# Delta net front: keys and queries side by side in one tile, one product of 256 columns for both

## The chip, the cores and the metric

The kernel runs on one core of a Trainium2 chip. Its time is the device time of one launch in microseconds (us): the median of three runs before the change is 1162.49 us (1161.85 to 1162.65). The engines of a core each run their own queue of instructions in order and wait for each other by semaphores: PE (matrix products), DVE (vector), ACT (scalar functions), POOL (GpSimd), SP (which issues DMAs here).

## What is computed

One residual block: a layer norm, a mixer of two branches with gates, a second norm, and a mixture of experts. The change lies in the second branch, a gated delta net with 8 heads of 128 channels over 512 positions. For each head, keys, queries and values are projections of the normed input, each through a causal convolution of four taps and a SiLU. The reference, cut to what matters here:

```
qkv = jax.nn.silu(_causal_dwconv(dn_qkv, dn_conv_w))
q, k, vv = jnp.split(qkv, [DN_KEY, 2 * DN_KEY], axis=-1)
...
kk = jnp.einsum('bhnik,bhnjk->bhnij', k, k)
lmat = jnp.where(strict, beta[..., :, None] * kk * decay, 0.0)
amat = jnp.eye(CHUNK) + lmat
sol = lax.linalg.triangular_solve(amat, rhs, left_side=True, lower=True, unit_diagonal=True)
attn = jnp.einsum('bhnik,bhnjk->bhnij', q, k) * decay
...
v_new = uu - ww @ state
o = qd @ state + aa @ v_new
state = state * cd + kd.T @ v_new
```

So two products have the keys as one factor: keys with keys, which gives the matrix to invert, and keys with queries, which gives the attention inside a chunk. The kernel takes chunks of 128 positions, four per head.

## The kernel before

The program is cut into parts whose instructions are recorded first and then put in order: the norm and the gated spatial branch with the decays; the delta net; the merge; then routing and the experts, which are written in their final order. The change touches the delta net alone.

In that part, `front(h)` prepares a head and `chain(h)` solves and steps through its chunks. The loop over heads records `front(h + 1)` and then `chain(h)`, so that one head is prepared while the other is stepped. Six gate projections for the merge are recorded behind everything (`gates_b`), and each has to follow the first operation of head 7's chain, which reads Lx and thus L:

```
rec.rank, rec.after, rec.after_on = 2 * H, rec.ops[first], ("PE", "ACT", "SP")
kk.gates_b(TG, range(2, 8))
```

A projection (`proj`) is 24 products of 128 x 512 named psi in the trace. Its weights come as one 512 KB transfer `raw`, which ACT rounds to `hi` and DVE subtracts to `lo`; of `raw` there are three buffers, of `hi` and `lo` two. `conv` copies the projection out (`xp`), multiplies and adds the taps (`acc`, three times on DVE), and ACT applies SiLU into `kT`, `qT` or `kr`.

`front` then, for the keys: transposes them (`pk<-ident,kT`, `tr4`), takes sums of squares (`ssk`), scales (`kd`), and computes factors on POOL (`rk`, `cb`, and the decay matrix `DL`). Four products `pkk` of keys with keys (in the trace pk<-kT) times DL give `L`. From L come Lx (four copies on POOL), Ld, Lc, Le on DVE, the product `pl` (pk<-Le), Lb on ACT, and fourteen short steps on DVE (pr and U8, both in the trace as pr and U) that invert blocks of 8, then U and Uc, and the transposition `pu` of Uc. Behind that in the record stand the queries: projection, convolution, transposition, ssq, rq, the products `paq` (pk<-qT,kT) and `aT`; last the values. `chain` doubles the inverted blocks (tiles B, pz, pt, Z, Tc, Ud, Td, then Z6 and T6), and then steps through four chunks: p1 (state with keys and queries), R, p2 with U, V, p4 with kd, Sn, p3 with aT (in the trace all p), o.

What sets the order is a planner: `Rec.order` runs through a list of all recorded operations, with a cost for each, and places on the engine that is free first what is ready, by rank (`2h + 2` for a front, `2h + 1` for a chain, one more for projections) and then by the place in the record. On PE it keeps to one kind, wide (projections) or not, while something of it is ready, with at most six wide ones in a row when another kind waits. Every engine then runs its own list in that order. PSUM has one bank for the front (pool PF, tag pf, in the trace pk), two for projections, two for pz and pt, three for the steps.

Of the kernel before, what the change touches and what calls it, by code (L numbers as in the profile page):

```python
# [16 lines left out]
F32 = mybir.dt.float32  # L17
# [4 lines left out]
AF = mybir.ActivationFunctionType  # L22
OP = mybir.AluOpType
# [27 lines left out]
C_BU, C_BQ, C_BK, C_BV, C_BZ, C_BGA, C_BGB = (8 * i for i in range(7))  # L51
# [9 lines left out]
def bc(ap, n, at):  # L61

    dims = [list(d) for d in ap.ap]
    dims.insert(at, [0, n])
    return bass.AP(tensor=ap.tensor, offset=ap.offset, ap=dims)
# [255 lines left out]
class K:  # L321
# [384 lines left out]
    def conv(self, W, ps, tileno, bcol, out):  # L706

        nc, c = self.nc, self.c
        col = lambda i: c["cols"][:, i:i + 1]
        xp = self.xp[self.nxp % 2]  # L710
        self.nxp += 1
        nc.scalar.activation(out=xp[:, 3:515], in_=ps, func=AF.Identity, bias=col(bcol))
        cw = C_CONV + 4 * tileno
        acc = W.tile([128, T], F32, name="acc")
        nc.scalar.activation(out=acc, in_=xp[:, 3:515], func=AF.Copy, scale=col(cw + 3))
        for j in (2, 1, 0):
            nc.vector.scalar_tensor_tensor(out=acc, in0=xp[:, j:j + 512], scalar=col(cw + j), in1=acc,
                                           op0=OP.mult, op1=OP.add)
        nc.scalar.activation(out=out, in_=acc, func=AF.Silu)

    def front(self, h, W, W1, PF):


        nc, c = self.nc, self.c
        v, act, te = nc.vector, nc.scalar, nc.tensor
        hc = lambda name: c[name][:, :, h]
        f2 = lambda t: t.rearrange("p j n -> p (j n)")

        def wide(name):
            return PF.tile([128, 4, 128], F32, name=name, tag="pf")  # L730

        def full(name, pool=W):
            return pool.tile([128, 4, 128], F32, name=name)
# [5 lines left out]

        base = 25 + 4 * h  # L740
        s = {"h": h}
        s["kT"] = kT = full("kT")
        self.conv(W, self.proj(base + 2), 8 + h, C_BK + h, f2(kT))
        pk = wide("pk")
        self.tr4(pk, kT)
        ssk = W.tile([128, 4], F32, name="ssk")
# [10 lines left out]
        s["nc"] = cb[:, 2]  # L757
        DL = self.DL[h]
        nc.gpsimd.tensor_tensor(out=DL, in0=DL, in1=bc(cb[:, 1], 128, 2), op=OP.mult)
        pkk = wide("pkk")  # L760
        for j in range(4):
            te.matmul(pkk[:, j], kT[:, j], kT[:, j], start=True, stop=True)
        s["L"] = L = full("L")
        v.tensor_tensor(out=L, in0=pkk, in1=DL, op=OP.mult)

        s["Lx"] = Lx = W.tile([128, 4, 32], F32, name="Lx")
        for i in range(4):
# [11 lines left out]
        Le = W1.tile([128, 4, 8, 8], F32, name="Le")  # L779
        v.tensor_tensor(out=Le, in0=bc(Lc, 8, 2), in1=bc(bc(c["del8"], 8, 2), 4, 1), op=OP.mult)  # L780
        pl = wide("pl")
        plf = f2(pl)[:, 0:256]
        te.matmul(plf, c["blk8"], Le.rearrange("p t i j -> p (t i j)"), start=True, stop=True)
        Lb = W1.tile([128, 4, 8, 8], F32, name="Lb")
        act.copy(out=Lb.rearrange("p t i j -> p (t i j)"), in_=plf)
# [2 lines left out]
        for j in range(7):  # L788
# [5 lines left out]
                        in1=bc(c["blk8"].rearrange("p (b i) -> p b i", i=8), 4, 1), op=OP.mult)  # L794
        s["Uc"] = Uc = W.tile([128, 4, 32], F32, name="Uc")
        v.tensor_tensor(out=Uc.rearrange("p t (b i) -> p t b i", i=8), in0=bc(U8, 4, 2),
                        in1=bc(c["blk8c"].rearrange("p (b i) -> p b i", i=8), 4, 1), op=OP.mult)
        pu = wide("pu")
        te.transpose(pu[:, 0], f2(Uc), c["ident"])
        s["Tc"] = Tc = W.tile([128, 128], F32, name="Tc")  # L800
        act.copy(out=Tc, in_=pu[:, 0])
        s["qT"] = qT = full("qT")
        self.conv(W, self.proj(base + 1), h, C_BQ + h, f2(qT))
        pq = wide("pq")
        self.tr4(pq, qT)
        ssq = W.tile([128, 4], F32, name="ssq")
# [2 lines left out]
        v.tensor_scalar(ssq, ssq, 128.0, 128.0 * L2_EPS, op0=OP.mult, op1=OP.add)  # L809
        s["rq"] = rq = W.tile([128, 4], F32, name="rq")  # L810
        nc.gpsimd.tensor_tensor(out=rq, in0=ssq, in1=c["mhalf"][:, 0:4], op=OP.pow)
        paq = wide("paq")
        for j in range(4):
            te.matmul(paq[:, j], kT[:, j], qT[:, j], start=True, stop=True)
        s["aT"] = aT = full("aT")
        v.tensor_tensor(out=aT, in0=paq, in1=self.DA[h], op=OP.mult)
        vr = full("kr")
        self.conv(W, self.proj(base), 16 + h, C_BV + h, f2(vr))
        pv = wide("pv")
        self.tr4(pv, vr)  # L820
        s["vb"] = vb = full("vb")
# [1159 lines left out]
def build(nc, tc, a):  # L1981
# [70 lines left out]
    TG = pool("tg")  # L2052
    PF, PW, PS = pool("pf", 1, space=PSUM), pool("pw", 2, space=PSUM), pool("ps", 1, space=PSUM)
    front, chain = (Static(HW, 2), Static(HW1), Static(PF)), (Static(PW, 2), Static(PS))
    kk.tgs = []
    st = kk.front(0, *front)
    rec.rank = 2.5
    kk.gates_b(TG, range(0, 2))
    for h in range(H):

        rec.rank = 2 * h + 2
        nxt = kk.front(h + 1, *front) if h + 1 < H else None
        rec.rank = 2 * h + 1
        first = len(rec.ops)
        kk.chain(st, *front, *chain)
        zeros.append(rec.sync.dma_start(out=y_dram[h * 128:(h + 1) * 128, :].rearrange("p (a n) -> p a n", a=4),
                                        in_=bc(zero, 4, 1)))
        st = nxt
# [192 lines left out]
```

## Time and profile before

| | |
|---|---|
| median of 3 runs | 1162.49 us (1161.85 to 1162.65) |
| time of the profiled execution | 1165.03 us |
| its span | 1163.2 us |
| PE busy | 1033.1 us (89%), 7046 products |
| DVE busy | 633.9 us (54%) |
| ACT busy | 369.2 us (32%) |
| POOL busy | 215.5 us (19%) |
| HBM read and written | 273.74 MB and 21.00 MB |

The profile is of one execution. A row of the timeline gives the start in us from the span's start, the duration, the engine, the line of the kernel (all recorded operations have one line, L275), the operation, the tile written and the tiles read, the part of PE's array, the shape, how many in a row, and in brackets how long the engine idled before it and what it waited for. Matmuls are pipelined, so that starts, not durations, tell what one costs; a product in 32-bit floats shows as two rows (two passes), a transposition and a psi as one. In a table of windows a row gives the stretch, its length, the busy time of PE, of PE's weight loads, DVE, ACT and POOL, the share of the clock that PE was granted, the DMA share and GB/s. In a group's row stand the count, the busy time and the mean in ns, and the idle time before.

### The profile page before, as it was taken

Reading aid. Unit: us, or ns where it says so; the run is one execution under the profiler, and the core shown is the slowest. Engines: PE = TensorE matmul, PEld = TensorE weight load, DVE = VectorE, ACT = ScalarE, POOL = GpSimd, SP = SyncE. Lnnn points to the kernel's source line nnn. Section 1 sums busy time; section 2 is a strip of 40 time slices with the busy share of each in tenths; the row PEclk is TensorE's granted clock in tenths of the full one; section 3 lists DMA queues with packets and bytes.
Section 4 is the critical chain, followed back from the end, with each engine's and each line's share of the span. In section 5 each row is a group of like instructions: output and inputs, shape, how many; then the busy total and the mean of one; then the engine's idle time right before and its main releaser. Section 6 shows DMA issues by size and latency. Waiting matters only on the chain. (4 is left out here: it accounts for less than half of the span.)

```text
span 1163.2 us, 18964 instructions
## 1 busy us (share of the span) xinstructions
PE 1033.1 (89%) x7046; PEld 684.4 (59%) x7046; DVE 633.9 (54%) x1435; ACT 369.2 (32%) x818; POOL 215.5 (19%) x291
## 2 busy tenths in 40 slices
PE   5999999999999999999999987798788787978754
PEld 4888788877777777777888753343333433333321
DVE  8575444477678677863485755354434432222156
ACT  6343346444544555443533122112111111110110
POOL 3010100032212222120100112224122222121110
PEclk9999999999999999998999999999999998998955
DMA  5412432711121121111647399999999999999996
GB/s 215 152 71 75 160 109 93 235 56 55 56 73 51 60 65 61 57 56 40 240 178 307 140 380 395 396 396 388 408 374 410 393 408 386 418 388 408 414 418 245
DMA packets 56210, 268.35 MB, mean 231 GB/s; under 512 B 10867, under 2 KB 15251, under 8 KB 32288
## 3 DMA queue, kind: packets, MB, share of 16 engines
q1 hardware_dynamic: 44400, 246.96, 55.4%
q0 software_dynamic: 9104, 14.87, 3.8%
q10 hardware_dynamic: 2592, 4.99, 1.2%
q8 instruction: 73, 1.20, 0.4%
q14 instruction: 41, 0.34, 0.1%
HBM read 273.74 MB, written 21.00 MB: 253 GB/s over the span
## 5 line engine op out<-in xcount | busy, mean ns | idle before, releaser
L275 PE MATMUL psi<-hTh,hi 128*128 128x512 f32 x448 | 184.8, 415 | 0.0
L275 PE MATMUL psi<-hTh,lo 128*128 128x512 f32 x448 | 180.8, 404 | 0.3 <-DVE lo L275 0.3
L275 PE MATMUL psi<-hTl,hi 128*128 128x512 f32 x448 | 180.6, 404 | 0.0
L275 DVE TENSOR_TENSOR lo<-raw,hi 128x1024 fp32r<-128x1024 f32 x74 | 92.5, 1250 | 75.2 <-ACT hi L275 75.0
L1768 PE MATMUL us<-raw,xs 128*32 128x256 f32 x1296 | 90.1, 418 | 33.5 <-DMA raw<-in_w 24.0
L1784 DVE TENSOR_TENSOR h<-h,us 128x128 f32<-128x128 f32 x32 | 9.2, 288 | 191.7 <-ACT h L1783 181.2
L275 ACT CAST hi<-raw 128x1024 fp32r<-128x1024 f32 x74 | 77.4, 1046 | 107.3 <-PE psi L275 89.3
L275 PEld LDWEIGHTS psi<-hTl,hi 128*128 128x128 f32 x448 | 84.7, 189 | 20.8 <-issue 3.0
L275 PEld LDWEIGHTS psi<-hTh,hi 128*128 128x128 f32 x448 | 84.8, 189 | 20.3 <-issue 3.3
L275 PEld LDWEIGHTS psi<-hTh,lo 128*128 128x128 f32 x448 | 85.0, 190 | 18.5 <-issue 1.8
L1768 PEld LDWEIGHTS us<-raw,xs 128*32 128x32 f32 x1296 | 42.6, 117 | 75.9 <-issue 25.5
L1768 PE MATMUL u<-raw,x 128*64 128x512 f32 x304 | 72.6, 620 | 10.0 <-PEq L1684 4.1
L1812 POOL DMA_INDIRECT y_rows<-once,itail x28 | 25.3, 903 | 240.5 <-DVE once L1832 207.6
L1783 ACT ACTIVATE h<-us 128x128 f32<-128x128 f32 x32 | 8.9, 277 | 187.2 <-PE us L1768 118.2
L275 DVE SCALAR_TENSOR_TENSOR acc<-xp,cols,acc 128x512 f32<-128x512 f32 x72 | 53.9, 749 | 5.3 <-ACT acc L275 4.3
L1793 ACT COPY hT<-t 128x128 f32<-128x128 f32 x32 | 8.5, 266 | 151.0 <-PE t L1790 144.1
L1768 PEld LDWEIGHTS u<-raw,x 128*64 128x64 f32 x304 | 22.8, 141 | 53.2 <-issue 49.5
L1832 DVE COPY once<-yz 32x256 f32<-32x256 f32 x112 | 46.7, 417 | 13.4 <-DMA y_rows<-once,itail 6.8
L1805 PE MATMUL yz<-raw,hT 128*32 128x256 f32 x576 | 43.8, 447 | 8.3 <-DMA raw<-in_w 5.5
L275 POOL TENSOR_TENSOR rk<-ssk,mhalf 128x4 f32<-128x4 f32 x8 | 10.0, 1251 | 177.9 <-DVE ssk L275 177.9
L1698 POOL DMA_INDIRECT mh<-h_dram,idx x36 | 35.1, 975 | 40.8 <-issue 22.6
L1805 PE MATMUL y<-raw,hT 128*64 128x512 f32 x160 | 38.0, 620 | 5.2 <-PEq L1684 2.4
(544 smaller groups left out, 1979.0 us busy)
## 6 DMA issues: line engine op xcount, KB each, us to landing
raw<-in_w SPq DMA_DIRECT2D x147, 1024.0 KB
raw<-in_wt SPq DMA_DIRECT2D x73, 512.0 KB
rawl<-in_w SPq DMA_DIRECT2D x22, 1024.0 KB
rawh<-in_w SPq DMA_DIRECT2D x22, 1024.0 KB
raw<-in_wv SPq DMA_DIRECT2D x8, 512.0 KB
y_rows<-zero SPq DMA_DIRECT2D x8, 512.0 KB
rawl<-in_wo SPq DMA_DIRECT2D x3, 1024.0 KB
vt<-in_x SPq DMA_DIRECT2D x4, 512.0 KB
```

Source lines behind the costliest of these rows:

```text
L275: op._ins = getattr(getattr(self.nc, op.attr), op.name)(*map(real, op.args), **{k: real(x) for k, x in op.kw.items()})
L1698: self.nc.gpsimd.indirect_dma_start(out=x, out_offset=None, in_=self.h1_dram, in_offset=bass.IndirectOffsetOnAxis(ap=self.blocks[b][2 + i] ...
L1768: self.nc.tensor.matmul((self.end if p is None else self.u[:, p])[q * r:(q + 1) * r, 0:c], x[:, k, r0:r0 + r], self.raw[b, k // 2][:, o:o ...
L1783: self.nc.scalar.activation(out=h, in_=u, func=AF.Silu)
L1784: self.nc.vector.tensor_mul(out=h, in0=h, in1=w)
L1793: self.nc.scalar.copy(out=x[:, n], in_=self.t[1][:, 0:128])
L1805: self.nc.tensor.matmul(y[q * r:(q + 1) * r, 0:c], t[:, i, j * r:(j + 1) * r], self.raw[b, 4 + k // 2][:, o:o + c], start=k == 0, stop=k == 3)
L1812: x = self.nc.gpsimd.indirect_dma_start(out=out, out_offset=bass.IndirectOffsetOnAxis(ap=idx, axis=0), in_=src, in_offset=None, bounds_che ...
L1832: nc.vector.tensor_copy(out=small[:, q], in_=src)
```

## The change

Keys and queries of a head become the two halves of one tile `kq` of four chunks by two by 128, so that `kT` and `qT` are views of it. The queries' projection and convolution are recorded ahead of L. The eight products of 128 columns (pkk and paq) become four of 256 columns, two chunks in each of two PSUM tiles `pkq`; DVE takes L and aT from their halves, two chunks at a time. `conv` writes its result through a view by chunk.

```
-        nc.scalar.activation(out=out, in_=acc, func=AF.Silu)
+        nc.scalar.activation(out=out, in_=acc.rearrange("p (j n) -> p j n", j=4), func=AF.Silu)
...
-        s["kT"] = kT = full("kT")
-        self.conv(W, self.proj(base + 2), 8 + h, C_BK + h, f2(kT))
+        kq = W.tile([128, 4, 2, 128], F32, name="kq")
+        s["kT"], s["qT"] = kT, qT = kq[:, :, 0], kq[:, :, 1]
+        self.conv(W, self.proj(base + 2), 8 + h, C_BK + h, kT)
...
-        pkk = wide("pkk")
-        for j in range(4):
-            te.matmul(pkk[:, j], kT[:, j], kT[:, j], start=True, stop=True)
+        self.conv(W, self.proj(base + 1), h, C_BQ + h, qT)
         s["L"] = L = full("L")
-        v.tensor_tensor(out=L, in0=pkk, in1=DL, op=OP.mult)
+        s["aT"] = aT = full("aT")
+        for i in (0, 2):
+            pkq = PF.tile([128, 2, 2, 128], F32, name="pkq", tag="pf")
+            for j in range(2):
+                te.matmul(pkq[:, j].rearrange("p a n -> p (a n)"), kT[:, i + j], kq[:, i + j].rearrange("p a n -> p (a n)"),
+                          start=True, stop=True)
+            v.tensor_tensor(out=L[:, i:i + 2], in0=pkq[:, :, 0], in1=DL[:, i:i + 2], op=OP.mult)
+            v.tensor_tensor(out=aT[:, i:i + 2], in0=pkq[:, :, 1], in1=self.DA[h][:, i:i + 2], op=OP.mult)
...
-        s["qT"] = qT = full("qT")
-        self.conv(W, self.proj(base + 1), h, C_BQ + h, f2(qT))
...
-        paq = wide("paq")
-        for j in range(4):
-            te.matmul(paq[:, j], kT[:, j], qT[:, j], start=True, stop=True)
-        s["aT"] = aT = full("aT")
-        v.tensor_tensor(out=aT, in0=paq, in1=self.DA[h], op=OP.mult)
```

The rest of the diff (the transposition and norm of the queries, the values) keeps its place in the record. The planner makes new lists for all engines out of it. Three places of them follow; numbers behind names tell buffers apart, and of two heads in flight the numbers of one are, before the change, kT_1688, qT_1699, U_1696, and after it kq_1687 and U_1696, both for head 7.

On PE before, the steps of head 6 and pk<-Le of head 7, up to the first psi of head 7's z projection (psi_153 with hi_203). The first product with U_1696 comes 25 rows later, behind 23 psi:

```order
L275 MATMUL psi_153<-hTl_68,hi_203 128x512
L275 MATMUL pk_1661<-Le_1672,blk8_166 128x256
L275 MATMUL p1_1721<-Sn_1725,kT_1659 128x128
L275 MATMUL p1_1721<-Sn_1725,qT_1679 128x128
L275 MATMUL p2_1716<-R_1726,U_1676 128x128
L275 MATMUL p4_1718<-V_1717,kd_1664 128x128
L275 MATMUL p2_1716<-V_1717,aT_1683 128x128
L275 MATMUL pk_1661<-ident_127,qT_1699 128x128
L275 MATMUL p1_1721<-Sn_1719,kT_1659 128x128
L275 MATMUL p1_1721<-Sn_1719,qT_1679 128x128
L275 MATMUL psi_153<-hTh_67,hi_203 128x512
```

On PE in the changed kernel, the same place. The three rows ahead of these are the last psi of head 7's z projection, p2<-R and the second pkq; psi_154 with hi_201 is the first of the gate projections:

```order
L275 MATMUL p4_1716<-V_1715,kd_1664 128x128
L275 MATMUL p2_1714<-V_1715,aT_1669 128x128
L275 MATMUL pk_1661<-ident_127,kq_1687 128x128
L275 MATMUL p1_1719<-Sn_1717,kq_1659 128x128 x2
L275 MATMUL pk_1661<-ident_127,kq_1687 128x128
L275 MATMUL p2_1714<-R_1720,U_1678 128x128
L275 MATMUL p2_1714<-V_1722,aT_1669 128x128
L275 MATMUL pk_1661<-Le_1674,blk8_166 128x256
L275 MATMUL pk_1661<-ident_127,kq_1687 128x128
L275 MATMUL pt_1706<-U_1696,B_1703 32x128 x4
L275 MATMUL pk_1661<-ident_127,Uc_1697 128x128
L275 MATMUL psi_154<-hTh_67,hi_201 128x512
```

The z projection has moved ahead of the second pkq, and one transposition stands between pk<-Le and pt<-U,B where 23 psi stood.

On DVE in the changed kernel, the end of the same path, from the last two steps of U8 to the lo parts of the first two gate projections:

```order
L275 TENSOR_TENSOR pr_1677<-Lb_1675,U8_1676 128x4
L275 TENSOR_TENSOR U8_1676<-U8_1676,pr_1677 128x4
L275 TENSOR_TENSOR U_1696<-U8_1676,blk8_166 128x512
L275 TENSOR_TENSOR Uc_1697<-U8_1676,blk8c_171 128x128
L275 TENSOR_TENSOR Z_1705<-pt_1706,in32_176 128x512
L275 TENSOR_TENSOR lo_202<-raw_199,hi_201 128x1024
L275 TENSOR_TENSOR lo_204<-raw_200,hi_203 128x1024
```

Before, the first of these two lo parts (lo_202) stood among the U8 steps, twelve rows ahead of U_1696; now it stands behind Z.

On PE in the changed kernel, some 45 rows earlier, where the z projection of head 7 takes over the buffers hi_203 and lo_204 from the projection before it; the first row is the last psi of that one, the last row the first psi of z:

```order
L275 MATMUL psi_153<-hTl_68,hi_203 128x512
L275 MATMUL pk_1661<-ident_127,kq_1687 128x128
L275 MATMUL p2_1714<-vb_1684,U_1678 128x128
L275 MATMUL pk_1661<-ident_127,kq_1687 128x128 x3
L275 MATMUL p4_1716<-V_1715,kd_1664 128x128
L275 MATMUL p2_1714<-V_1715,aT_1669 128x128
L275 MATMUL p1_1719<-Sn_1717,kq_1659 128x128 x2
L275 MATMUL psi_153<-hTh_67,hi_203 128x512
```

On ACT at that place, the hi part of z's weights and the V that p4 reads:

```order
L275 COPY T6_1711<-pt_1706 64x256
L275 ACTIVATE U_1678<-pz_1704 64x4x64
L275 CAST yh5_3962<-z_1728 128x512
L275 CAST hi_203<-raw_198 128x1024
L275 COPY V_1715<-p2_1714 128x128
```

The buffers change hands here at the start of head 6's steps; before, that stood at pk<-Le and the steps of head 6's third and fourth chunk, which the first of these pieces shows.

More of the change, by code (lines that the diff above doesn't have):

```diff
@@ L726, in front @@
         hc = lambda name: c[name][:, :, h]
-        f2 = lambda t: t.rearrange("p j n -> p (j n)")
         def wide(name):
@@ L781, in front @@
         pl = wide("pl")
-        plf = f2(pl)[:, 0:256]
+        plf = pl.rearrange("p j n -> p (j n)")[:, 0:256]
         te.matmul(plf, c["blk8"], Le.rearrange("p t i j -> p (t i j)"), start=True, stop=True)
@@ L798, in front @@
         pu = wide("pu")
-        te.transpose(pu[:, 0], f2(Uc), c["ident"])
+        te.transpose(pu[:, 0], Uc.rearrange("p j n -> p (j n)"), c["ident"])
         s["Tc"] = Tc = W.tile([128, 128], F32, name="Tc")
         act.copy(out=Tc, in_=pu[:, 0])
-        s["qT"] = qT = full("qT")
-        self.conv(W, self.proj(base + 1), h, C_BQ + h, f2(qT))
         pq = wide("pq")
@@ L811, in front @@
         nc.gpsimd.tensor_tensor(out=rq, in0=ssq, in1=c["mhalf"][:, 0:4], op=OP.pow)
-        paq = wide("paq")
-        for j in range(4):
-            te.matmul(paq[:, j], kT[:, j], qT[:, j], start=True, stop=True)
-        s["aT"] = aT = full("aT")
-        v.tensor_tensor(out=aT, in0=paq, in1=self.DA[h], op=OP.mult)
         vr = full("kr")
-        self.conv(W, self.proj(base), 16 + h, C_BV + h, f2(vr))
+        self.conv(W, self.proj(base), 16 + h, C_BV + h, vr)
         pv = wide("pv")
```

## The prediction

> **What bounds the kernel now.** I read the busy time by stage first, cut at the points where the program's parts change: the delta net (215 to 566 us), the merge and routing (to 681), the experts (to the end).
>
> ```profile
> core 0: us, PE busy (x) PEld busy (x) DVE busy (x) ACT busy (x) POOL busy (x), PEclk, DMA share, GB/s
> 215.00:566.00 351.00, 343.57 (x2069) 267.28 (x2069) 237.66 (x535) 168.70 (x446) 78.70 (x120) 0.99 0.23 73
> 566.00:681.00 115.00, 114.47 (x606) 91.73 (x609) 81.11 (x205) 39.42 (x47) 7.94 (x9) 1.00 0.63 245
> 681.00:1163.00 482.00, 373.68 (x3464) 165.00 (x3456) 192.55 (x442) 64.49 (x153) 107.73 (x118) 0.89 0.99 389
> ```
>
> In the stage that the diff touches PE is busy for 343.57 of 351.00 us. It idles for 7.43 us, and everything else has room (DVE 68%). So the end of this stage is its start, plus the PE work in it, plus what PE waits. The next stage is PE's as well (114.47 of 115). The experts are bound by transfers (DMA share 0.99), and their loads into buffers begin when the stages ahead let buffers go and the chain of waits ends in these loads. A microsecond of the delta net is therefore a microsecond of the kernel.
>
> Next I read where PE waits, in its timeline. These are its waits around the last head (number 7):
>
> ```profile
> 506.06 0.59 PE L275 MATMUL pk<-Le,blk 128*128 128x256 f32 x2
> 507.55 0.49 PE L275 MATMUL p<-R,U 128*128 128x128 f32 x2 [0.45 <-DVE R L275]
> 508.39 0.49 PE L275 MATMUL p<-V,kd 128*128 128x128 f32 x2 [0.36 <-ACT V L275]
> 508.94 0.27 PE L275 MATMUL pk<-ident,qT 128*128 128x128 f32 x1
> 509.32 0.49 PE L275 MATMUL p<-Sn,kT 128*128 128x128 f32 x2
> ...
> 516.36 0.38 PE L275 MATMUL pt<-U,B 128*32 128x128 f32 x2 [0.51 <-POOL r L275]
> ...
> 528.50 0.66 PE L275 MATMUL pz<-Z,Td 128*64 128x128 f32 x8 [0.45 <-DVE Z L275]
> 530.10 0.41 PE L275 MATMUL pz<-ident,U 64*64 64x64 f32 x4 [0.94 <-DVE U L275]
> ```
>
> With 0.11 at 509.32 (the row before it ends at 509.21) they make 2.8 us of idle, and since a wait also loses the overlap of one product with the next (about 0.15 each), some 3.7 us lost. The other seven heads have the remaining 4.6 us of idle in 14 waits, or 6.9 us lost.
>
> **The product.** What 128 and 256 columns cost stands in one run without a wait:
>
> ```profile
> 353.28 0.39 PE L275 MATMUL psi<-hTh,hi 128*128 128x512 f32 x1
> 353.51 0.38 PE L275 MATMUL p<-Sn,kT 128*128 128x128 f32 x2
> 353.73 0.39 PE L275 MATMUL p<-Sn,qT 128*128 128x128 f32 x2
> 353.95 0.60 PE L275 MATMUL pk<-Le,blk 128*128 128x256 f32 x2
> 354.20 0.58 PE L275 MATMUL psi<-hTh,lo 128*128 128x512 f32 x1
> 354.62 0.39 PE L275 MATMUL psi<-hTl,hi 128*128 128x512 f32 x1
> ```
>
> A 128-column product (two passes) takes 0.22 us from start to start. The 256-column one takes 354.62 - 353.95 less one psi (353.51 - 353.28, 0.23): 0.44. Per head, eight at 0.22 become four at 0.44: 1.76 both ways. The weight loads were hidden already, so halving them saves **nothing**. Bounds: 0.5 us less over all heads if the 256-column pass streams a little better, and 3.4 more if each of the 32 products pays the 0.1 that such a product shows behind a wait. I take 0, the row without a wait. The planner prices them at 180 and 243 ns (in its cost function), so it places the work as if the product had become cheaper.
>
> DVE gets four operations of 256 columns for two of 512. Its nearest rows, grouped over the stage:
>
> ```profile
> L275 DVE TENSOR_TENSOR Ud<-Uc,half 128x256 f32<-128x256 f32 x8 | 3.3, 418 | 0.0
> L275 DVE TENSOR_TENSOR o<-o,r 128x512 f32<-128x512 f32 x8 | 5.5, 687 | 0.1
> ```
>
> So 4 x 0.42 for 2 x 0.69, 0.3 us more per head, on an engine with a third of its time free. PE and DVE share one PSUM bank here, so the second pkq waits for two of these reads (0.85 us); six psi (1.4 us) or more stand between the two in every head. Cost 0; without the cover 0.85 per head.
>
> **The order.** Products on a part of the array (128*32, 128*64, 64*64) cost more to enter and leave: 0.21 into such a group and 0.20 + 0.34 out of it, against 0.11 and 0.03 + 0.32.
>
> ```profile
> 518.77 0.27 PE L275 MATMUL pk<-ident,qT 128*128 128x128 f32 x1
> 518.98 0.43 PE L275 MATMUL pz<-Z,Tc 128*32 128x128 f32 x8
> 519.33 0.50 PE L275 MATMUL psi<-hTl,hi 128*128 128x512 f32 x1
> 519.67 0.40 PE L275 MATMUL psi<-hTh,hi 128*128 128x512 f32 x1
> ```
>
> That is 0.28 us a group. Counted in the order, the shape changes 141 times before and 150 times now, some 4.5 groups more: **+1.3 us** (bounds 0 and 2.5).
>
> The large term is at head 7. L now needs the queries, so k's and q's projections both run before it, and fewer psi are left behind it. By the order the z projection of head 7 is used up before the second pkq, and the last gate projections (they are recorded behind the first operation of head 7's chain, which needs L) come after pt<-U,B. Between the second pkq and pt<-U,B stand ten short products and **no psi**. The latencies of what PE then waits for:
>
> ```profile
> 502.61 0.69 DVE L275 TENSOR_TENSOR L<-pk,DL 128x512 f32<-128x512 f32 x1
> 503.37 1.31 POOL L275 COPY Lx<-L 32x128 f32<-32x128 f32 x4 [0.79 <-DVE L L275]
> 505.47 0.43 DVE L275 TENSOR_TENSOR Le<-Lc,del 128x256 f32<-128x256 f32 x1
> ...
> 238.82 0.70 PE L275 MATMUL pk<-Le,blk 128*128 128x256 f32 x2 [0.43 <-DVE Le L275]
> 239.55 0.37 ACT L275 COPY Lb<-pk 128x256 f32<-128x256 f32 x1 [0.29 <-PE pk L275]
> 240.36 0.44 DVE L275 TENSOR_TENSOR pr<-Lb,U 128x28 f32<-128x28 f32 x1
> 244.63 0.38 PE L275 MATMUL pz<-U,B 128*32 128x128 f32 x2 [0.34 <-DVE U L275]
> ```
>
> Let the clock start with p2<-R, the row ahead of the second pkq. It ends at 0.22 + 0.88 + 0.16 (drain) = 1.26. The second half of L takes 0.42, to 1.7; from the end of L to the end of Le is 505.90 - 503.30 = 2.6 us, so pk<-Le starts at 4.35. Lb stands on ACT behind a sum of squares that waits for the last p2<-V, and starts at 5.2 (0.2 late); pr starts at 5.6. From the first pr to the first product with U are 4.27 us (head 0, nothing between). Here r3 (0.15) and o (0.69) stand between, so pt<-U,B starts near 10.7. PE's own work until there is seven products of 128 columns (p1, p2, p4: 1.5), three transpositions of one pass (0.3), pkq (0.88) and pk<-Le (0.44): 3.2 us. **7.5 us are lost.** Right behind it the first gate projection needs its lo part, which stands on DVE behind Z (0.69, which itself waits for pt<-U,B), 1.2 us long: another 0.8. Queued behind the waiting pt<-U,B on PE are the transposition of Uc, all gate projections and the rest of head 7's chain; nothing else has work to go on with. Bounds: the 5.5 us from pk<-Le to pt<-U,B less 0.4 of work if all else is hidden, and 10.
>
> A smaller hole stands ahead of it, where the z projection of head 7 takes the weight buffer of the projection before. Its hi part is on ACT after U and yh and ahead of V; its lo part is on DVE ahead of Sn:
>
> ```profile
> 506.26 1.05 ACT L275 CAST hi<-raw 128x1024 fp32r<-128x1024 f32 x1 [2.03 <-PE psi L275]
> 507.41 1.22 DVE L275 TENSOR_TENSOR lo<-raw,hi 128x1024 fp32r<-128x1024 f32 x1
> ```
>
> p4<-V, with no psi ahead of it, comes 1.2 us late behind the 1.05 of hi, and p1<-Sn another 0.8 late behind the 1.22 of lo: **+2.0** (bounds 0 and 3). Before, the same change of buffers fell on the waits at 507.55 to 509.32.
>
> Those waits (3.7 us) go: in the new order six psi stand between the last steps of head 7 where one or none stood. In heads 0 to 6 the order has, between pk<-Le and the first use of U, 5.1, 8.1, 6.0, 7.6, 6.0, 7.9 and 5.8 us of PE work (before 5.3 to 9.5) for a path of 5.8 us (238.82 to 244.63) that DVE's other work lengthens. I expect 3.3 us of waits there, 2.7 elsewhere, against 6.9: **-0.9** (bounds -5 and +3).
>
> **The clock.** PE's granted clock halves after a stretch in which it idled much:
>
> ```profile
> 528.06:531.47 3.41, 2.03 (x22) 1.61 (x23) 2.98 (x5) 3.12 (x7) 0.00 (x0) 1.00 0.00 0
> 531.47:534.88 3.41, 3.41 (x15) 2.35 (x14) 0.00 (x0) 0.49 (x3) 0.00 (x0) 0.50 0.47 154
> 534.88:538.30 3.42, 3.42 (x10) 2.74 (x11) 0.00 (x0) 0.48 (x2) 0.00 (x0) 0.50 0.00 0
> 265.23:268.64 3.41, 2.27 (x11) 1.46 (x11) 2.78 (x6) 3.32 (x7) 3.14 (x5) 1.00 0.00 0
> ```
>
> After 2.03 us busy of 3.41 came 6.8 us at half clock (about 3.3 us lost); after 2.27 of 3.41 none. The new hole leaves a whole such window nearly empty, so the half clock should come with it, after it or partly inside it, and the one at 531.47 should go, as its cause does. I take 0 (bounds -3.3 and +3.4). [...]
>
> **Sum**: 0 + 1.3 + 7.5 + 0.8 + 2.0 - 3.7 - 0.9 + 0 = +7.0 us. The profiled execution took 1165.03 us (span 1163.2), 2.5 over the median of the runs, so it would become 1172, and the median 1162.49 becomes **1169.5**.
>
> **The rivals.**
> 1. *The hole is paid for by waits that go.* The early queries take their projection, convolution and transpositions out of each head's later part. If heads 0 to 6 then lose 1.5 us instead of 6.9 and the hole is the 5.1 of its lower bound, with the small one closed: 1.3 + 5.1 - 3.7 - 5.4 = -2.7, and -6 if the half clock at 531.47 goes unreplaced: 1157 to 1160. It decides if those heads lose under 2 us. Against it speak the covers of 5.8 to 6.0 us above, which are no longer than the bare path. This is the faster side. 0.10.
> 2. *They cancel.* The holes open, but the half clock goes without a new one (-3.3) and the other heads gain their -3: about 1.3 + 10.3 - 3.7 - 3 - 3.3 = +1.6, 1164. 0.12.
> 3. *The wide product is cheap.* If a pass of 256 columns took half of psi's 0.23 for 512, a product would be 0.23 for 0.44, 0.8 us less per head and 6.6 in all: +0.4, 1163. The row at 353.95 speaks against it: its two passes take 0.44. 0.03. [...]
> 4. *Worse.* The half clock lasts longer than two windows, or the U paths of three more heads wait 1 to 2 us behind convolutions on DVE: +11 to +12, 1174. 0.10.
> 5. *My forecast*, +4 to +10: 0.65.
>
> That the product does not come out as one of 256 columns is excluded by the order.
>
> **How the numbers follow.** A measurement of this kernel can tell about 0.2%, 2.3 us, from no change. Faster by more: rival 1, 0.10. Within it: rivals 2 and 3, 0.15. Slower by more: 4 and 5, 0.75. The range leaves out rival 1 and a part of rival 4: 1161.5 to 1174.5.
>
> **What would show it.** In the changed profile PE should idle 5 to 6 us in one piece before pt<-U,B in the last head, released by DVE's U, with ACT's V and DVE's Sn late some 10 us before; PEclk 0.50 in the next window or two; the pairs of kq passes 0.44 apart; no waits like those at 528 and 530; and the later stages moved as a whole. I am wrong if PE's total idle in this stage stays near 7 us, if the 256-column products come under 0.4, or if the experts' transfers start no later although the delta net ends later.

## The result, and the profile after

The changed kernel takes 1173.70 us (median of 5 runs, 1170.76 to 1176.59) where the kernel before takes 1162.49 (5 runs, 1161.85 to 1163.74): a ratio of 1.0094, with a 95% interval of 1.0078 to 1.0109. It is 0.9% slower, 11 us; the forecast was 7. Its profiled execution took 1176.44 us (span 1174.6), 11.4 more than the profiled one of before. Of all runs below one was slow, 1180.84 us in e7_all, and it is left out of that kernel's median and ratio.

The windows of the changed kernel, cut 11 us later than those of before since its stages end later, with the columns as in the prediction:

```profile
215.00:577.00 362.00, 348.91 (x2018) 266.90 (x2017) 243.01 (x552) 171.03 (x448) 78.55 (x120) 0.98 0.22 72
577.00:692.00 115.00, 113.53 (x623) 90.37 (x622) 82.97 (x218) 40.32 (x49) 8.65 (x10) 1.00 0.65 252
692.00:1174.00 482.00, 377.22 (x3428) 165.80 (x3426) 190.52 (x429) 62.39 (x150) 107.48 (x117) 0.87 0.98 386
```

PE's idle in the delta net has gone from 7.43 to 13.09 us. The first product us<-raw of the experts starts at 689.17 where it started at 681.34: **+7.8 us come from the delta net**. The end is 11.4 us later, so 3.6 more arise among the experts.

The timeline of PE in the changed kernel, at the last head, from p2<-R to the first gate projection (rows left out at "..."):

```profile
516.92 0.38 PE L275 MATMUL p<-R,U 128*128 128x128 f32 x2
517.14 1.03 PE L275 MATMUL pk<-kq 128*128 128x256 f32 x4
...
520.10 0.49 PE L275 MATMUL p<-R,U 128*128 128x128 f32 x2 [0.24 <-DVE R L275]
520.94 0.49 PE L275 MATMUL p<-V,aT 128*128 128x128 f32 x2 [0.35 <-ACT V L275]
521.27 0.69 PE L275 MATMUL pk<-Le,blk 128*128 128x256 f32 x2
522.50 0.33 PE L275 MATMUL pk<-ident,kq 128*128 128x128 f32 x1 [0.55 <-ACT Lb L275]
526.97 0.65 PE L275 MATMUL pt<-U,B 128*32 128x128 f32 x8 [4.13 <-DVE U L275]
...
530.00 0.47 PE L275 MATMUL pk<-ident,kr 128*128 128x128 f32 x1 [0.56 <-ACT junk L275]
530.13 0.78 PE L275 MATMUL psi<-hTh,lo 128*128 128x512 f32 x1
```

This is the forecast hole. From p2<-R to pt<-U,B are 10.05 us, with no psi in between. DVE in the same stretch shows the chain that PE waits for:

```profile
518.21 0.42 DVE L275 TENSOR_TENSOR L<-pk,DL 128x256 f32<-128x256 f32 x1 [1.81 <-PE pk L275]
...
520.78 0.42 DVE L275 TENSOR_TENSOR Le<-Lc,del 128x256 f32<-128x256 f32 x1
...
522.68 0.19 DVE L275 TENSOR_TENSOR pr<-Lb,U 128x28 f32<-128x28 f32 x1
...
524.31 0.68 DVE L275 TENSOR_TENSOR o<-o,r 128x512 f32<-128x512 f32 x1
...
526.13 0.69 DVE L275 TENSOR_TENSOR U<-U,blk 128x512 f32<-128x512 f32 x1
...
528.28 2.35 DVE L275 TENSOR_TENSOR lo<-raw,hi 128x1024 fp32r<-128x1024 f32 x2
```

From pr to U they are one short step behind the other, with o (0.68) of the head before among them; lo follows behind. The first of its two operations takes 1.22 us and ends at 529.50, ahead of the psi at 530.13 that reads it: the 0.56 us of idle before 530.00 are a wait for ACT's sum of squares (junk), which stands behind a hi (528.22 to 529.27). PE's half clock around it, in windows of 3.41 us (in both profiles the stretches of one granted clock are multiples of that length, but for the last; the shortest at 0.50 are one of it):

```profile
264.37:267.78 3.41, 1.88 (x12) 1.17 (x10) 2.68 (x2) 2.83 (x6) 1.66 (x3) 1.00 0.00 0
267.78:271.19 3.41, 3.41 (x12) 2.84 (x11) 0.58 (x2) 0.80 (x3) 0.00 (x0) 0.50 0.48 154
520.37:523.78 3.41, 1.56 (x7) 0.76 (x6) 2.45 (x10) 1.95 (x6) 3.15 (x5) 1.00 0.01 2
523.78:527.19 3.41, 0.22 (x6) 0.23 (x8) 2.99 (x13) 0.00 (x0) 0.07 (x1) 0.50 0.00 0
527.19:530.61 3.42, 2.87 (x21) 1.39 (x14) 2.93 (x4) 1.95 (x7) 0.00 (x0) 0.50 0.03 5
530.61:534.02 3.41, 3.41 (x14) 2.40 (x16) 1.30 (x5) 0.73 (x5) 1.01 (x1) 0.50 0.81 279
534.02:537.43 3.41, 3.41 (x29) 2.38 (x23) 2.14 (x6) 0.43 (x2) 0.00 (x0) 1.00 0.06 24
```

Before there was one half clock of 6.83 us; now there are 3.41 at 267.78 and 10.24 at 523.78, a part of it empty. The account of the stage, from the first transposition of keys to the first us<-raw, worked out from the trace: idle is the sum of PE's gaps, half clock is half of the busy time at 0.50 (there a psi takes 0.43 us from start to start, 530.70 to 531.13 in the changed kernel, and 0.23 at full clock, 534.59 to 534.82), and the rest is work at full clock with the overlaps lost.

| kernel | stage | idle | half clock | rest |
|---|---|---|---|---|
| before | 456.5 | 8.0 | 3.4 | 445.1 |
| changed | 464.3 | 13.6 | 5.0 | 445.8 |
| difference | +7.9 | +5.7 | +1.5 | +0.7 |

The other 3.6 us were not forecast. The timeline of PE at the first expert of the changed kernel:

```profile
689.17 1.05 PE L1766 MATMUL us<-raw,xs 128*32 128x256 f32 x16
690.56 0.64 PE L1766 MATMUL us<-raw,xs 128*32 128x256 f32 x8 [0.34 <-PEq L1599]
691.79 0.38 PE L1766 MATMUL us<-raw,xs 128*32 128x256 f32 x1 [0.59 <-DVE x L1713]
695.93 1.08 PE L1766 MATMUL us<-raw,xs 128*32 128x256 f32 x7 [3.76 <-issue]
697.17 1.94 PE L1766 MATMUL us<-raw,xs 128*32 128x256 f32 x16 [0.17 <-DMA raw<-in_w]
699.98 2.83 PE L1766 MATMUL u<-raw,x 128*64 128x512 f32 x6 [0.87 <-DVE se L1360]
```

Between the first and the second of eight equal products PE stands for 3.76 us and waits for nothing that the profile shows ("issue"). Before, the eight stand together, and the first u<-raw follows:

```profile
684.14 0.64 PE L1768 MATMUL us<-raw,xs 128*32 128x256 f32 x8 [0.79 <-PEq L1665]
...
688.50 5.32 PE L1768 MATMUL u<-raw,x 128*64 128x512 f32 x16 [2.48 <-DVE den L1365]
```

From the first us<-raw to the first u<-raw it is 10.81 us in the changed kernel and 7.17 before; from there to the end it is 474.7 in both. So all of the 3.6 us are lost at this place. The window 691.04 to 694.45 then has PE busy for 0.54 us, and 10.24 us at half clock follow. The transfers fall from 384 GB/s in the 58.66 us from the first us<-raw on to 361. Among the trace's transfers of the kind "instruction" (1.18 MB in 72 pieces of 16 KB) one runs from 693.55 to 694.56, inside the stop.

### The profile page after: what moved, and what is told of

The parts are those of the page before. It is cut to its first block, busy times and chain, and to the rows that moved or that the text cites. A ratio compares the mean times of both kernels' runs of the same rounds, so it can differ in the third digit from the quotient of the medians.

```text
span 1174.6 us, 18851 instructions
## 1 busy us (share of the span) xinstructions
PE 1040.8 (89%) x6982; PEld 683.3 (58%) x6982; DVE 638.8 (54%) x1451; ACT 370.4 (32%) x818; POOL 215.8 (18%) x291
## 3 DMA queue, kind: packets, MB, share of 16 engines
q8 instruction: 72, 1.18, 0.4%
## 5 line engine op out<-in xcount | busy, mean ns | idle before, releaser
L275 PE MATMUL psi<-hTh,lo 128*128 128x512 f32 x448 | 183.5, 410 | 0.7 <-DVE lo L275 0.7
L1766 PE MATMUL us<-raw,xs 128*32 128x256 f32 x1296 | 93.7, 430 | 30.6 <-DMA raw<-in_w 22.1
L1766 PE MATMUL u<-raw,x 128*64 128x512 f32 x304 | 75.3, 640 | 8.3 <-PEq L1682 4.4
L1782 DVE TENSOR_TENSOR h<-h,u 128x512 f32<-128x512 f32 x16 | 11.0, 689 | 55.5 <-ACT h L1781 55.5
```

The costliest lines, as they stand in the source:

```text
L275: op._ins = getattr(getattr(self.nc, op.attr), op.name)(*map(real, op.args), **{k: real(x) for k, x in op.kw.items()})
L1766: self.nc.tensor.matmul((self.end if p is None else self.u[:, p])[q * r:(q + 1) * r, 0:c], x[:, k, r0:r0 + r], self.raw[b, k // 2][:, o:o ...
L1782: self.nc.vector.tensor_mul(out=h, in0=h, in1=w)
```

## The experiments

The theories. **Order**: L waits for the queries, the wide work runs out before the last head, and the hole, the small hole and the half clock follow. **Product**: 256 columns are dearer or cheaper than twice 128. **Spread**: later inversions cost in every head, whatever the order. And, formed on the traces of e1_gates_early and e2_narrow, **code place**: the stop at the first expert depends on where the pieces of PE's program begin. A ratio is to runs of before beside it; the last two columns (us) are of the profiled execution.

| run | median us (runs) | ratio (95%) | first us<-raw | stop there |
|---|---|---|---|---|
| changed kernel | 1173.70 (5) | 1.0094 (1.0078 to 1.0109) | 689.2 | 3.76 |
| e1_gates_early | 1171.16 (6) | 1.0058 (1.0038 to 1.0077) | 684.3 | 3.76 |
| e2_narrow | 1173.32 (6) | 1.0077 (1.0061 to 1.0092) | 690.6 | none |
| e3_query_first | 1162.24 (12) | 0.9994 (0.9981 to 1.0007) | 679.5 | none |
| b1_gates_early | 1160.39 (7) | 0.9969 (0.9956 to 0.9981) | 675.9 | none |
| pad_after | 1171.60 (6) | 1.0070 (1.0049 to 1.0091) | 687.9 | none |
| pad_before | 1164.15 (12) | 1.0006 (0.9988 to 1.0024) | 682.5 | 2.37 |
| e1n_gates_early_narrow | 1167.93 (12) | 1.0043 (1.0029 to 1.0058) | 684.5 | none |
| b2_query_first_gates_early | 1159.71 (12) | 0.9970 (0.9958 to 0.9982) | 675.9 | none |
| e6_true_cost | 1167.09 (12) | 1.0029 (1.0017 to 1.0042) | 682.4 | 1.89 |
| b4_true_cost | 1162.10 (12) | 0.9986 (0.9975 to 0.9997) | 678.4 | none |
| b3_gates_earlier | 1160.63 (12) | 0.9972 (0.9960 to 0.9984) | 675.8 | none |
| e7_all | 1165.06 (11) | 1.0004 (0.9990 to 1.0019) | 679.1 | none |

### The gates earlier, in the changed kernel

```
-        first = len(rec.ops)
+        firsts.append(len(rec.ops))
...
-    rec.rank, rec.after, rec.after_on = 2 * H, rec.ops[first], ("PE", "ACT", "SP")
+    rec.rank, rec.after, rec.after_on = 2 * H, rec.ops[firsts[H - 2]], ("PE", "ACT", "SP")
```

> The changed kernel with one edit: the last six gate projections are recorded behind the first operation of head 6's chain, not of head 7's, so that the planner may place them earlier; by the order 17 wide products then stand between pk<-Le and pt<-U,B of the last head, where none stood. Theory (the loss is the hole before pt<-U,B, the small one at the buffer turnover, and the half clock that follows them): PE's idle in the delta net falls from 13 us to 7 or less, no half clock longer than 3.4 us at the end of the stage, and the time falls by 6 to 10 us, to 1163 to 1168. Rival A (the queries' early place, the extra tile-shape changes or the product itself cost it, spread over all heads): the hole closes but the time stays within 2 us of the changed kernel's 1174. Rival B (the experts' stage alone makes the difference, by where in its phase it starts): the delta net ends earlier and the end of the kernel does not follow.

Its timeline of PE at the last head (psi rows without a wait left out):

```profile
523.75 0.60 PE L275 MATMUL pk<-Le,blk 128*128 128x256 f32 x2
...
526.80 0.49 PE L275 MATMUL p<-V,aT 128*128 128x128 f32 x2 [0.97 <-ACT V L275]
...
530.20 0.41 PE L275 MATMUL pt<-U,B 128*32 128x128 f32 x2
...
538.27 0.49 PE L275 MATMUL psi<-hTh,hi 128*128 128x512 f32 x1 [0.83 <-ACT tgb L275]
```

The hole is closed: no wait stands before pt<-U,B, and the long half clock is gone. The first expert starts 4.8 us earlier (idle -3.8, half clock -3.3, rest +2.3). But smaller waits remain, idle stays at 9.8 us rather than 7, and the time falls by 2.5 us (by the ratios 4) instead of 6 to 10. Only part of the theory is borne out: the stop of 3.76 us is in this kernel as well, and the 2.3 us of the rest have no account. What the same edit gains in the kernel before follows below.

### The same order, with narrow products

```
                 op = te.matmul(pkq[:, j]...)
+                op.parts = [((pkq[:, j, a], kT[:, i + j], kq[:, i + j, a]), op.kw) for a in range(2)]
```

Each part is issued as a product of its own, so that the order is unchanged.

> The changed kernel with the same order on every engine, but each product of 256 columns issued as two of 128 (keys with keys, keys with queries), back to back. It tells what the width itself is worth. Theory (the width is neutral): within 1 us of the changed kernel, 1172 to 1175, and the start-to-start time of a pair 0.44 in both. Rival (a wide product is cheaper, 0.05 to 0.1 us each, 32 products): 1.7 to 3.4 us slower than the changed kernel. Rival (a wide product is dearer): 1.7 to 3.4 us faster.

The same place in the timeline of PE, first the changed kernel, then this one:

```profile
356.18 1.03 PE L275 MATMUL pk<-kq 128*128 128x256 f32 x4
357.05 0.38 PE L275 MATMUL p<-R,U 128*128 128x128 f32 x2
```

```profile
356.05 1.06 PE L275 MATMUL pk<-kq 128*128 128x128 f32 x8
356.94 0.39 PE L275 MATMUL p<-R,U 128*128 128x128 f32 x2
```

Two wide products take 0.87 us from start to start, four narrow ones 0.89: 0.01 a product, not 0.05 to 0.1. By these rows the theory that the width is neutral holds. The time, within 0.4 us of the changed kernel's, can't tell it alone, for two differences stand against each other in it: the stage is 1.4 us longer (465.8 us; with the gates early, e1n_gates_early_narrow against e1_gates_early, 0.2), and the stop at the first expert is gone, although nothing of the experts was touched.

### The queries early without the dependency, and the gates early in the kernel before

The queries' projection and convolution are moved ahead of pkk in the kernel before; products stay narrow and separate. The second run is the edit of the first experiment, on the kernel before.

```
+        s["qT"] = qT = full("qT")
+        self.conv(W, self.proj(base + 1), h, C_BQ + h, f2(qT))
         pkk = wide("pkk")
```

> The kernel before with only the queries' projection and convolution recorded ahead of the products of keys with keys, which stay narrow and separate, so that L does not wait for the queries. By the order 24 wide products stand between pk<-Le and pt<-U,B of the last head. Theory (it is the dependency of L on the queries, through the shared tile and the place of pkq, that makes the hole): no idle above 1 us in the last head before pt<-U,B, and 1161 to 1166. Rival A (recording the query projection ahead already costs it, since L comes later in the planner's order too): 1168 to 1174.

> The kernel before with the last six gate projections recorded behind the first operation of head 6's chain instead of head 7's; nothing else. It tells whether the kernel before already paid for the late gates: its waits of the last head (some 3.7 us) and its half clock at 531 to 538 (some 3.3 us). Theory: if both come from running short of wide products at the end, 1156 to 1161; rival: the gates are used up earlier and the end of the chain is left bare, the same waits come back later, 1161 to 1168.

PE in the first of them, before the first product with U of the last head:

```profile
516.09 0.38 PE L275 MATMUL pt<-U,B 128*32 128x128 f32 x2 [0.53 <-POOL r L275]
```

No hole, and the time of before. So it is not the early queries that cost. What is left by elimination is that L waits for them, through the shared tile; the half-width operations on DVE and the earlier place of aT were not separated from that. The gates early gain 0.3% (2.9 us) in the kernel before: its half clock at 531 goes, and idle falls from 8.0 to 5.9 us. What the order at the end costs, the kernel before had paid in part already. And by the ratios this edit gains about as much here (0.31%) as in the changed kernel (0.36%): it closes the hole, but it brings the two kernels hardly closer. Both runs come out as their theories said.

### The place of PE's code

The change takes 64 passes out of PE's program, 64 loads and 64 products (7046 of each in the profile before, 6982 in the changed one). Between fetches of 16 KB, PE went through 257 loads and products on average (20 stretches of the delta net and merge of before, 192 to 320 each), so 128 are half a piece. Two runs add 64 transpositions of the identity at the very start, where PE waits for the first input; one issues the early gates' kernel with narrow products.

```
+            self.pad = getattr(self, "pad", None) or op.name == "transpose" and [
+                self.nc.tensor.transpose(op.args[0], op.args[2], op.args[2]) for _ in range(64)]
```

> The changed kernel with 64 more transpositions of the identity at the very start, where PE waits some 10 us for the first input; they are overwritten, and the order of everything else is the same. They add 128 instructions to PE's program (a weight load and a product each), as many as the change took out of it. Theory: of the 11 us some 8 are lost in the delta net, and the rest in the experts' stage, where PE stops for 3.76 us inside its first expert while a 16 KB piece of its own instructions is fetched, and the half clock follows; where that piece begins depends on the number of instructions ahead of it. Then here no such stop near 690 us, the delta net's end unchanged (within 0.5 us of 575.0), and 1170 to 1172.5 where the changed kernel has 1173.7. Rival (the stop belongs to the stage's start time, to the transfers or to chance, not to the place in the program): the stop stays, and the time stays within 1 us of the changed kernel's.

> The kernel before with the same 64 transpositions of the identity at its very start, which shift its PE program by 128 instructions, to where the changed kernel's lies (modulo 256, the instructions that 16 KB hold at 64 bytes each, a size worked out from the fetches in the trace and not otherwise shown). Theory (the place in the program makes the stop): a pause of some 3 to 4 us inside the first expert's products near 682 us, with a 16 KB fetch in it, nothing changed in the delta net, and 1164.5 to 1167.5. Rival (start time, transfers or chance): no such pause, and within 1 us of before.

> The changed kernel with the gates early (as in the first experiment) and each product of 256 columns issued as two of 128, so that PE's program has as many instructions as before. With the gates early the delta net ended 6 us sooner than in the changed kernel, and yet the time fell by 2 to 3 us only; its trace has the same 3.76 us stop in the first expert. Theory (two separate losses: the hole, and the stop by the place of the code): the stop is gone and the time is 1166 to 1169. Rival (the experts' stage takes back what the delta net gains, whatever the code): 1170 to 1172, as with the gates early alone.

The first expert on PE in the padded changed kernel:

```profile
689.27 0.64 PE L1766 MATMUL us<-raw,xs 128*32 128x256 f32 x8 [0.33 <-PEq L1599]
690.62 0.64 PE L1766 MATMUL us<-raw,xs 128*32 128x256 f32 x8 [0.71 <-PEq L1663]
691.43 1.07 PE L1766 MATMUL us<-raw,xs 128*32 128x256 f32 x16 [0.17 <-PEq L1663]
```

and in the padded kernel before:

```profile
683.88 0.64 PE L1768 MATMUL us<-raw,xs 128*32 128x256 f32 x8 [0.33 <-PEq L1601]
685.10 0.38 PE L1768 MATMUL us<-raw,xs 128*32 128x256 f32 x1 [0.58 <-DVE x L1715]
687.85 0.64 PE L1768 MATMUL us<-raw,xs 128*32 128x256 f32 x7 [2.37 <-issue]
```

The padding takes the stop out of the one and puts it into the other, behind the same product. The fetches beside it, from the trace's transfers:

```
kernel           stop of PE          16 KB fetch of instructions
changed          692.17 to 695.93    693.55 to 694.56
e1_gates_early   687.33 to 691.09    688.61 to 689.67
pad_before       685.48 to 687.85    685.33 to 686.30
e6_true_cost     685.62 to 687.51    685.23 to 686.27
```

Of the 14 kernels these four have it, and these four alone have their code 128 instructions from its place before: three have 128 fewer ahead of it, pad_before has 128 more, and the two places are 256 apart, about the 257 of a fetch. A fetch alone does not make it: in all 14 one starts 2.8 to 4.4 us after the first us<-raw. What differs is the fetch ahead of that one, 12.5 to 13.7 us before the first us<-raw in the four and 4.7 to 5.2 in the others. So the place in the program decides, in one profiled execution of each; how the fetch holds PE up is not shown.

Its price in the profiled executions can be read at the place: from the first us<-raw to the first u<-raw it is 10.8 us in the two kernels with 3.76, 8.6 and 8.4 in pad_before and e6_true_cost, and 7.2 to 7.5 in the ten others; from there to the end it is 473 to 476 in all. The medians are less sharp. With and without it the ratios are 1.0094 and 1.0070 (padding) or 1.0077 (narrow), 1.0058 and 1.0043, and 1.0006 and 1: 0.7 to 2.8 us, each with intervals about as wide as itself.

Against the expectations: pad_after and e1n_gates_early_narrow come out as their theories said. In pad_before the pause comes, but "nothing changed in the delta net" does not hold (the half clock at its end lasts 10.24 us instead of 6.83, with the same order), and the time is in the rival's "within 1 us". In e1n_gates_early_narrow's text the 6 us are 4.8 at the first us<-raw. A second stop of the kind, 1.9 to 3.2 us long before a transposition t of a later expert, is in eight of the kernels, the changed one among them and the kernel before not, and was not followed.

In the delta net and the merge of the changed kernel 19 fetches of 16 KB start between 228 and 649 us, and none of PE's waits from 224 to 690 us is an "issue"; at the first expert of the four one is.

### The queries early and the gates early together

> The kernel before with the queries' projection and convolution recorded early (narrow, separate products; L does not wait for them) and the gates behind the first operation of head 6's chain: the two edits that cost nothing or gained alone. Theory (the gain of the gates, some 3 us, comes from the head-7 waits and the half clock at the end, and the early queries neither add nor take): 1158.5 to 1161, like the gates alone (1160.4). Rival (the early queries free the end of each head, so that both add up): under 1158.5. Rival (they compete for the same projections at the end): over 1161.

1159.71 us, ratio 0.9970: as the gates alone. The early queries add nothing and take nothing, and this version and the gates alone beat both kernels.

### The planner's prices

```
-            return max(180, 0.95 * n), max(386, 2.3 * n)
+            return max(220, 1.7 * n), max(386, 2.3 * n)
```

> The changed kernel; only the planner's price of a product of 32-bit floats is set to what the trace shows, 220 ns for 128 columns and 435 for 256 (it had 180 and 243). All engines get new lists: by the order of PE, 25 wide products stand between pk<-Le and the first product with U of the last head, where the changed kernel has none. Theory (the hole is a matter of the order that comes out, and the planner let the z projection and the gates run out too early because it took the wide products for half as long as they are): the idle before pt<-U,B of the last head falls under 1 us, the half clock of 10 us at the end goes, and the time is 1161 to 1167. Rival (L depends on the queries, so that every head's inversion starts later, whatever the prices): the waits come back in other places and the time is 1168 to 1174.

> The control to it: the kernel before with the same prices in the planner. Theory (the prices mattered for the change, since it replaced eight products priced 180 by four priced 243): the kernel before moves by less than 3 us, 1160 to 1165. Rival (true prices help any order alike): it falls by as much as the changed kernel, to 1155 or less.

PE in the changed kernel with true prices, at the last head:

```profile
512.99 0.60 PE L275 MATMUL pk<-Le,blk 128*128 128x256 f32 x2
...
522.53 0.33 PE L275 MATMUL pk<-ident,Uc 128*128 128x128 f32 x1 [0.48 <-DVE Uc L275]
522.78 0.43 PE L275 MATMUL pt<-U,B 128*32 128x128 f32 x8
```

The planner now puts psi between pk<-Le and pt<-U,B by itself; 0.48 us of waiting are left of the hole, and the 10 us of half clock are gone. The time falls from a ratio of 1.0094 to 1.0029, while the kernel before gains 0.0014 by the same prices (1162.10, as its theory said). The 1167.09 lie at the edge between the two expectations, and the code stop (1.89) is in it. So about half of the loss (0.65 of 0.94%, less the 0.14 that before gains too: 0.51, give or take 0.23 by the intervals) goes with the prices. Products entered at 243 ns take 435 (0.87 us for two, from 356.18 to 357.05), and by my reading the plan's PE ran ahead of the real one; no run shows that, and none separates the price of 256 columns from that of 128, which rose from 180 to 220 in the same edit.

### Two heads earlier still

> The kernel before with the early queries and the gates behind the first operation of head 4's chain (two heads earlier still than in b2_query_first_gates_early, 1159.7). Theory (the waits of the last head are gone already, and the gates taken earlier are missing nowhere): 1158 to 1161. Rival (more waits in heads 5 and 6 are covered): under 1158. Rival (the gates run out before the end and the last head waits): over 1161.

1160.63: nothing more to gain from placing the gates earlier still; the theory holds.

### All repairs together

The changed kernel with the true prices, the gates early and the padding.

> The changed kernel with all three repairs: true prices of the 32-bit products in the planner (220 and 435 ns), the gates behind the first operation of head 6's chain, and the 64 transpositions of the identity at the start that move the place of PE's code. Theory (the change itself, the wide product and the early queries, is worth nothing; all it cost came from the order and the place of the code): no stop in the first expert, no idle over 1 us in the last head, and 1160 to 1164, equal to before (1163.5 in the calls so far) and no better than the kernel before with early queries and gates (1159.7). Rival (L's dependency on the queries costs whatever the order): 1165 or more. Rival (side by side, the wide product has a gain that the order hid): under 1159.

1165.06, with before at 1164.05 beside it: ratio 1.0004 (0.9990 to 1.0019). There is no stop. One wait of 1.14 us remains in the last head, where the theory had none over 1 us:

```profile
528.38 0.66 PE L275 MATMUL pt<-U,B 128*64 128x128 f32 x8 [1.14 <-DVE U L275]
```

The changed kernel has come back to the time of the kernel before, but with repairs of which two help that kernel too. So the fair comparison is with the same repair in both (stage as in the account above, in us):

| repair | ratio, changed and before | difference | stage, changed and before | difference |
|---|---|---|---|---|
| none | 1.0094 and 1 | 0.94% | 464.3 and 456.5 | 7.9 |
| gates early | 1.0058 and 0.9969 | 0.89% | 459.5 and 451.1 | 8.5 |
| gates early, no stop (narrow) | 1.0043 and 0.9969 | 0.74% | 459.7 and 451.1 | 8.7 |
| true prices | 1.0029 and 0.9986 | 0.43% | 456.8 and 452.8 | 4.0 |
| all; before with early queries and gates | 1.0004 and 0.9970 | 0.34% | 455.1 and 451.1 | 4.0 |

In the last row the intervals do not touch (0.9990 to 1.0019 against 0.9958 to 0.9982), though before has no true prices and no padding there; no run has all three in the kernel before. The changed kernel's stage has 8.3 us of idle there against 5.9, no half clock in either, and 446.8 us of rest against 445.1. So the theory that the change itself is worth nothing is not borne out: at least some 4 us of its loss stayed in every order tried. The first rival, that L's dependency on the queries costs whatever the order, is not refuted; no run separates it from the changes of shape and the lost overlaps that are in the rest. What the 4 us are stays open. A gain of the wide product (the second rival) did not come up.

## Why the prediction was right, and where it was not

The sign and the main cause were right: the stage lost 7.9 us against a forecast of 7.0, and the largest piece of it is the hole before pt<-U,B. The whole, 11.2, lies above the forecast's own +4 to +10 and at rival 4's +11 to +12, which had 0.10. That rival's condition on the clock came true (three windows at half clock), but it is not what made 11 out of 7: the clock cost 1.5 us more than before, and the stop at the first expert, which neither foresaw, 3.6 in the profiled execution. That 1173.70 still lies under the range's 1174.5 is luck in that part.

- *The product, 0*: right, 0.87 against 0.89 us for the same work. The wait of the second pkq for PSUM was hidden too: 0.2 us in all.

```profile
L275 PE MATMUL pk<-kq 128*128 128x256 f32 x64 | 17.3, 392 | 0.2 <-DVE aT L275 0.2
```

- *Shapes, +1.3*: the rest of the account rose by 0.7, lost overlaps included. The term was about twice too large, as far as the rest tells it apart.
- *The hole, +7.5 and +0.8*: 10.05 us from p2<-R to pt<-U,B where 10.7 were worked out; less the 3.2 of PE's own work, 6.8 were lost. pk<-Le came 4.35 us after p2<-R, as worked out; from the first pr to pt<-U,B it was 4.29 where 4.27 for the path and 0.84 for r3 and o had been added up. The last piece alone is 4.13, not 5 to 6, since 1.14 of idle fell into three waits ahead of it. The 0.8 for lo did not come: lo was ready in time, and the 0.56 us of idle at that place are for ACT's sum of squares.
- *The small hole, +2.0*: two waits of 0.77 and 0.59, some 1.7 with the overlaps, 18 us ahead of the large hole and not some 10. PE first, then ACT and DVE, where hi and lo stand ahead of V and Sn as worked out:

```profile
507.50 0.49 PE L275 MATMUL p<-V,kd 128*128 128x128 f32 x2 [0.77 <-ACT V L275]
508.80 0.71 PE L275 MATMUL p<-Sn,kq 128*128 128x128 f32 x4 [0.59 <-DVE Sn L275]
```

```profile
506.24 1.05 ACT L275 CAST hi<-raw 128x1024 fp32r<-128x1024 f32 x1
507.19 0.26 ACT L275 COPY V<-p 128x128 f32<-128x128 f32 x1
```

```profile
507.32 1.23 DVE L275 TENSOR_TENSOR lo<-raw,hi 128x1024 fp32r<-128x1024 f32 x1 [0.25 <-ACT hi L275]
508.46 0.28 DVE L275 COPY Sn<-p 128x128 f32<-128x128 f32 x1
```

- *The waits of head 7, -3.7*: gone, as said.
- *Heads 0 to 6, -0.9*: the wrong sign. Their idle went from 4.6 us to 5.8 (12 waits, the longest 0.84 before pt<-U,B of head 3 and 0.81 before p<-vb,U of head 0). With 0.15 a wait for the overlap (an estimate, from products that last 0.38 us and start 0.22 apart) that is 7.6 us lost, where before had 6.7 (4.6 and 14 times 0.15; the prediction's 6.9 is a slip). The step that failed is "I expect 3.3 us of waits there, 2.7 elsewhere", and in it the second number. Between pk<-Le and the first use of U five waits make 2.4 us of idle, 3.2 with the overlaps, as expected; elsewhere seven make 3.4, or 4.4.
- *The clock, 0*: +1.5. The one at 531 was replaced by the longer one, as said; a second came in head 0, after a window with 1.88 us busy.
- *"The later stages moved as a whole"*: wrong. They moved by 7.8 and lost 3.6 more in the profiled execution. The step that failed is "A microsecond of the delta net is therefore a microsecond of the kernel": PE's code had become shorter as well, and with its new place in the program came the stop at the first expert. By the medians of the padded and narrow runs the stop is 0.7 to 2.8 us of the 11. What the step says of the work itself is shown in part: in the two rows of the table above without the stop, stage and time differ alike (8.7 us and 0.74%, 4.0 us and 0.34%), but in b1_gates_early 5.4 us less of the stage came out as 2.9 less of the median, and the profiled execution of before had lain 2.5 over its median.

So the sum of 7.0 was low by 0.9 in its own stage, partly by errors that cancel, and the rest of the way to 11 is the stop and its half clock.

## What to carry to other kernels

Where a planner places instructions from a table of prices, the prices need to be measured before a change is judged: here about half of the loss went when they were. Give each repair to the kernel before as well, for a repair that helps both says nothing of the change: the gates placed early closed the hole and left the difference as it was. Ask of each edit which long latency now starts later and what independent work is still left behind it; the last turn of a loop has the least. And look at long "issue" rows: here a change of PE's instruction count far ahead brought a stop into a stage that the change did not touch.

## What the runs showed of the hardware

- A stop of 1.9 to 3.8 us of PE beside a 16 KB instruction fetch while the data transfers go on (354 GB/s from 691.04 to 694.45 in the changed kernel), brought in or taken out by 128 instructions added some 680 us earlier.
- In the delta net the clock halved after windows with 1.88 and 1.56 us busy of 3.41 (before: after 2.03, not after 2.27). It returned after one full busy window in the changed kernel (267.78 to 271.19; 530.61 to 534.02, behind two with 0.22 and 2.87 busy) and after two before (531.47 to 538.30); in pad_before, which has the order of before, the half clock lasted 10.24 us (528.89 to 539.13).
